# A two-layer hybrid DeltaNet trunk on one core: TensorE's order in the mixer fixed to the program's, the merges of two heads in lockstep, and the second short convolution ahead of the third head

## The chip, the cores and the metric

The kernel runs on one core of a Trainium2 chip. The metric is the device time of one execution in microseconds (us); the time given for a kernel is the median of several executions. A profile is one execution of the program, recorded instruction by instruction.

## What is computed

The trunk has two layers over 1024 positions of width 1024, all in float32. Cut to what matters here:

```python
def hybrid_layer(x, ...):
    h = rms_norm(x, norm1_g)
    proj = h @ w_in
    qkv, z, b_in, a_in, sc_in = ...split of proj...
    qkv = silu(causal_depthwise_conv(qkv, dn_conv_w))
    q, k = l2_normalize(q), l2_normalize(k)          # 4 heads of 128
    ...
    o_dn = chunk_gated_delta_rule(q, k, v, g, beta)  # a triangular solve per chunk, a scan over chunks
    o_dn = o_dn * rsqrt(mean(o_dn^2)) * dn_norm_g * silu(z)
    y = gate_b * causal_depthwise_conv(gate_c * hv, sc_conv_w)   # 4 groups of 128 channels
    o_sc = rms_norm over each group of y
    x = x + concatenate([o_dn, o_sc]) @ w_out
    h2 = rms_norm(x, norm2_g)
    return x + (silu(h2 @ ffn_w_gate) * (h2 @ ffn_w_up)) @ ffn_w_down
```

## The kernel before

**Matrix products.** Everything is held with channels on the 128 partitions and positions along the free axis, in two halves of 512 positions (half 0 and half 1). A float32 product is made of three passes: each operand is split into a rounded part `hi` (a copy on ScalarE) and the remainder `lo` (a subtraction on VectorE or GpSimd), and `mm3` (L205) issues hi·hi, hi·lo and lo·hi for each of the 8 slices of the 1024 input channels. One projection of 128 output channels over one half is 24 TensorE instructions of 128x512.

**One layer.** The mixer projects k, q and v for head 0 to 3 (`ps_k`, `ps_q`, `ps_v`), then z (`ps_z`, the gate of a head's output) and the three inputs of each short convolution group (`sconv`: `ps_csc`, `ps_hsc`, `ps_bsc`). Then come the output projection (`po`), gate and up (`P_g`, `P_u`), down (`P_d`), and a tail (`pd`) that adds the last four slices of the down projection.

**The delta rule beside the projections.** Its steps are small products of 128x128 and less. They are written as generators, "jobs": `tick()` is called behind every projection matmul, counts each job's lag down by one and, at zero, lets it trace its next step (`move`). For a head: transposes of k and q to tokens (`ktok`, `qtok`, L507), the Gram products `gk` and `gq` (L583, evacuated by VectorE as `U` and `A` in L584), the scaling of `kdec` by a decay (L588), and the transposes of v (`vtok`). For a group of two heads: `invert` inverts 32x32 triangles on VectorE or GpSimd over DRAM; after a further `INV_LAG` ticks `merge` (L639 to L663: `rp32`, `yp32`, `rp64`, `yp64`) makes 128x128 inverses `Y` from them, half by half and head by head; `chain` (L687 to L712) scans the chunks of both heads side by side: `kS`, `TR`, `SU` and the outputs `op`, with VectorE and ScalarE evacuating between; and the gate (L752) multiplies by z and stores to DRAM (`od`). The last steps of a group have no ticks left to wait for where the projections have run out: `drain()` then traces them at once.

**The output projection's operands.** For each half, eight tiles `ot` are loaded back from `od` (L1030, on SyncE's queue), the four of the short convolutions are scaled by `rb` (L1034), and each is split into `hhi_o` (L1035, ScalarE) and `hlo_o` (L1036, VectorE). `ot` takes the four SBUF buffers of tag `q`, which also hold the heads' q.

**What sets the order.** A scheduler orders each engine's instructions by the program's order and by when it thinks that their inputs are ready. `tc.issue_after(i)` keeps what is traced under it behind instruction `i`; before, only the jobs are under it, each behind the last projection matmul traced so far. So a projection may pass the jobs, and does. PSUM has eight banks: two for the projections (`mm`), `aux` and `fx` for transposes, Gram products and merges, `ch0` and `ch1` for the chain's short products, `o0` and `o1` for its outputs `op`.

## Time and profile before

| | |
|---|---|
| three executions | 2421.8, 2418.4 and 2419.73 us, median 2419.73 us |
| the profiled execution | 2423.16 us, of which the span of the trace is 2421.5 us |
| mean granted clock of TensorE | 0.987 |
| TensorE busy | 2340.7 us (97%) of the span |
| VectorE, ScalarE, GpSimd busy | 1622.2, 910.3 and 602.3 us (67%, 38%, 25%) |
| layer 0: mixer, `po`, gate and up, down, tail | begin at 4.8, 462.6, 552.8, 987.4 and 1166.1 us |
| layer 1: the same, and the end | begin at 1217.2, 1650.9, 1741.3, 2175.3 and 2353.8 us; ends at 2421.5 us |

The 1.66 us between the profiled execution's time and its span lie outside the trace. The stages' times are those of the first TensorE instruction of each.

### The profile page before, as it was taken

How to read it: one execution, taken by the hardware profiler on the slowest of the kernel's cores; microseconds unless marked ns; L12 is line 12 of the kernel's file. 1: busy time of each engine (PE TensorE's matmuls, PEld its weight loads, DVE VectorE, ACT ScalarE, POOL GpSimd, SP SyncE). 2: the span in 40 equal slices, each digit the busy share in tenths (PEclk: the TensorE clock that was granted, in tenths of full speed). 3: DMA queues.
4: the chain of work that ended last, by engine and by line, in shares of the span. 5: the costliest groups of instructions: out<-in, count | busy, mean ns of one | idle time of the engine just before them, and what ended most of it. 6: DMA issues, size and time to landing. Idle time of an engine off the chain costs nothing.

```text
span 2421.5 us, 31888 instructions
## 1 busy us (share of the span) xinstructions
PE 2340.7 (97%) x11522; PEld 1908.2 (79%) x11522; DVE 1622.2 (67%) x2870; ACT 910.3 (38%) x1917; POOL 602.3 (25%) x492
## 2 busy tenths in 40 slices
PE   7999999999999999999998999999999999999998
PEld 5787787887788888788777778878878888887877
DVE  7775773767655655799776666646685565568994
ACT  5524523534323223443344244234342322334334
POOL 3000000031444433234221001000325443422350
PEclk8999999999999999999999999999999999999999
DMA  7222223652333323744322312338423332346531
GB/s 228 66 65 71 65 63 90 204 183 61 109 118 105 113 87 98 248 144 146 106 69 71 76 49 69 77 92 251 124 75 119 106 113 87 109 137 220 160 101 70
DMA packets 362167, 275.21 MB, mean 114 GB/s; under 512 B 47343, under 2 KB 295449, under 8 KB 362009
## 3 DMA queue, kind: packets, MB, share of 16 engines
q1 hardware_dynamic: 362008, 273.18, 37.4%
q8 instruction: 90, 1.47, 0.3%
q14 instruction: 69, 0.56, 0.1%
HBM read 198.08 MB, written 75.04 MB: 113 GB/s over the span
## 4 chain that ended last, share of the span: by engine, by line
PE 73%; DVE 12%; issue 6%; DMA 4%; POOL 3%; ACT 2%; SPq 0%; DVEq 0%; POOLq 0%; ACTq 0%
PE P_g L205 16%; PE P_u L205 14%; PE P_d L205 7%; PE po L205 5%; PE ps_csc L205 4%; PE ps_bsc L205 4%; PE ps_hsc L205 4%; PE pd L205 3%; PE ps_v L205 3%; PE ps_z L205 2%; PE ps_k L205 2%; PE ps_q L205 2%; DMA stP<-hs_P 2%; DMA row<-gd 2%; DVE xT L1237 1%
## 5 line engine op out<-in xcount | busy, mean ns | idle before, releaser
L205 PE MATMUL P_g<-hi_hP,hi_P_g 128*128 128x512 f32 x608 | 239.5, 394 | 3.4 <-DVE u_g L995 1.9
L205 PE MATMUL P_g<-lo_hP,hi_P_g 128*128 128x512 f32 x608 | 238.7, 393 | 3.6 <-DVE lo_hP L898 3.6
L205 PE MATMUL P_u<-hi_hP,hi_P_u 128*128 128x512 f32 x608 | 237.6, 391 | 3.1 <-DVE c_g L1011 2.2
L205 PE MATMUL P_u<-lo_hP,hi_P_u 128*128 128x512 f32 x608 | 237.3, 390 | 0.0
L205 PE MATMUL P_u<-hi_hP,lo_P_u 128*128 128x512 f32 x608 | 237.1, 390 | 0.0
L205 PE MATMUL P_g<-hi_hP,lo_P_g 128*128 128x512 f32 x608 | 236.4, 391 | 0.0
L205 PE MATMUL P_d<-hi_dP,lo_P_d 128*128 128x512 f32 x504 | 196.8, 390 | 3.3 <-DVE lo_P_d L928 3.3
L205 PE MATMUL P_d<-hi_dP,hi_P_d 128*128 128x512 f32 x504 | 196.7, 390 | 2.2 <-ACT hi_dP L897 1.5
L205 PE MATMUL P_d<-lo_dP,hi_P_d 128*128 128x512 f32 x504 | 196.6, 390 | 0.9 <-DVE lo_dP L898 0.9
L205 PEld LDWEIGHTS P_g<-hi_hP,hi_P_g 128*128 128x128 f32 x608 | 114.9, 189 | 30.6 <-DVE u_g L995 2.8
L205 PEld LDWEIGHTS P_g<-lo_hP,hi_P_g 128*128 128x128 f32 x608 | 115.0, 189 | 28.7 <-DVE lo_hP L898 5.2
L205 PEld LDWEIGHTS P_u<-hi_hP,hi_P_u 128*128 128x128 f32 x608 | 114.6, 189 | 28.5 <-DVE c_g L1011 3.1
L205 PEld LDWEIGHTS P_g<-hi_hP,lo_P_g 128*128 128x128 f32 x608 | 114.9, 189 | 23.7
L205 PEld LDWEIGHTS P_u<-lo_hP,hi_P_u 128*128 128x128 f32 x608 | 114.7, 189 | 23.9
L205 PEld LDWEIGHTS P_u<-hi_hP,lo_P_u 128*128 128x128 f32 x608 | 114.4, 188 | 23.7
L1237 DVE TENSOR_TENSOR xT<-P_d,xT 128x512 f32<-128x512 f32 x192 | 125.1, 678 | 3.1 <-PE P_d L205 3.1
L927 ACT CAST hi_P_g<-m_g 128x1024 fp32r<-128x1024 f32 (+1 forms) x64 | 58.8, 919 | 151.9 <-PE P_u L205 127.7
L205 PEld LDWEIGHTS P_d<-hi_dP,lo_P_d 128*128 128x128 f32 x504 | 94.6, 188 | 25.0 <-DVE lo_P_d L928 5.8
L205 PEld LDWEIGHTS P_d<-hi_dP,hi_P_d 128*128 128x128 f32 x504 | 94.6, 188 | 23.6 <-ACT hi_dP L897 2.8
L205 PEld LDWEIGHTS P_d<-lo_dP,hi_P_d 128*128 128x128 f32 x504 | 94.6, 188 | 21.8 <-DVE lo_dP L898 2.2
L898 DVE TENSOR_TENSOR lo_dP<-stP,hi_dP 128x512 fp32r<-128x512 f32 x126 | 96.6, 790 | 18.0 <-ACT hi_dP L897 17.8
L897 ACT CAST hi_dP<-stP 128x512 fp32r<-128x512 f32 x126 | 75.2, 620 | 74.4 <-DMA stP<-hs_P 71.0
(410 smaller groups left out, 5872.0 us busy)
## 6 DMA issues: line engine op xcount, KB each, us to landing
stP<-hs_P SPq DMA_DIRECT2D x126, 256.0 KB, 3.8
m_g<-in_ffn_w_gate_dram SPq DMA_DIRECT2D x46, 512.0 KB, 4.1
m_u<-in_ffn_w_up_dram SPq DMA_DIRECT2D x44, 512.0 KB, 4.4
hs_P<-t SPq DMA_DIRECT2D x72, 256.0 KB, 2.4
m_d<-in_ffn_w_down_dram SPq DMA_DIRECT2D x48, 384.0 KB, 4.1
hs_P<-c_u SPq DMA_DIRECT2D x70, 256.0 KB, 2.0
raw_o<-in_w_out_dram SPq DMA_DIRECT2D x32, 512.0 KB, 4.8
xd<-xT SPq DMA_DIRECT2D x32, 256.0 KB, 2.3
```

The costliest lines, as they stand in the source:

```text
L205: last_mm[0] = PE.matmul(ps, lhsT=w(k)[i], rhs=m(k)[j], start=k + i + j == 0, stop=k + i == n).ins
L897: S.copy(res[0], src)
L898: eng.tensor_tensor(res[1], src, res[0].bitcast(F32), ALU.subtract)
L927: S.copy(hi, src)
L1237: V.tensor_tensor(t, ps, t, ALU.add)
```

## The change

In order of the diff: `LAG` goes from 6 to 8 and `INV_LAG` from 110 to 175 ticks, and tag `X` of the merges has two buffers. `mm3` puts each projection behind what was last traced on TensorE, and `move` does the same for each job, so that inside the mixer TensorE's order is the one in which the program traces it; only the first three projections of the kernel are free. For heads 0 and 1, whose work stands before any chain is running, `ktok`, `qtok`, `gk` and `gq` take the chain's banks `ch0`, `ch1`, `o0`, `o1` in place of `aux` and `fx`. The scaling of `kdec` moves from one VectorE instruction of 128x512 to four ScalarE activations of 128x128. The merges of a group's two heads go step by step side by side, one in `aux` and one in `fx`, and those of half 1 run beside the chain of half 0. The second short convolution comes before head 2. In the tail the splits of the down projection's weights are traced ahead of `tail_half(1)`, behind the last ScalarE copy of a split so far.

```diff
-LAG, TOK_LAG, SC_LAG, INV_LAG, GATE_LAG = 6, 36, 30, 110, 30
+LAG, TOK_LAG, SC_LAG, INV_LAG, GATE_LAG = 8, 36, 30, 175, 30
...
-    PB = {"tb": 1, "X": 1, "R": 2, "vn0": 1, "vn1": 1, "St": 6}
+    PB = {"tb": 1, "X": 2, "R": 2, "vn0": 1, "vn1": 1, "St": 6}
...
-    last_mm = [None]
+
+    last_mm, behind, strict = [None], [None], [True]
...
-                last_mm[0] = PE.matmul(ps, lhsT=w(k)[i], rhs=m(k)[j], start=k + i + j == 0, stop=k + i == n).ins
+                with tc.issue_after(behind[0]) if tick and behind[0] else nullcontext():
+                    mm = PE.matmul(ps, lhsT=w(k)[i], rhs=m(k)[j], start=k + i + j == 0, stop=k + i == n).ins
+                last_mm[0] = mm
+                behind[0] = mm if k + i == n and strict[0] else None
...
+            def side(hd, free, tag):
+
+                return lambda name, shape: ps_(free if hd < 2 else tag, name, shape)
...
             def move(job):
-                with tc.issue_after(last_mm[0]):
+                traced = nc.cur_bb.bb.instructions
+                n = len(traced)
+                with tc.issue_after(behind[0] or last_mm[0]):
...
+                for i in traced[n:]:
+                    if i.engine == last_mm[0].engine:
+                        behind[0] = i
...
+                strict[0] = l + hd + half > 0
...
-                ktok = transposed(u["k"], f"ktok_{nm}", aux)
+                ktok = transposed(u["k"], f"ktok_{nm}", side(hd, "ch0", "aux"))
...
-                V.tensor_tensor(u["kdec"], u["kdec"], u["kd"].unsqueeze(2).broadcast_to(sh4), ALU.mult)
+                for c in range(4):
+                    S.activation(u["kdec"][:, c, :], u["kdec"][:, c, :], AF.Copy, scale=u["kd"][:, c:c + 1])
...
-                vtok = transposed(u["v"], f"vtok_{nm}", aux)
+                vtok = transposed(u["v"], f"vtok_{nm}", (fx if hd < 2 and half else aux))
...
+                def merges(half):
+
+                    its = [merge(2 * g + i, half, i * 2 + half, (aux, fx)[i]) for i in range(2)]
+                    for lags in zip_longest(*its):
+                        yield LAG
+                yield from merges(0)
+                spawn(merges(1), 2 * LAG)
+                yield LAG
                 for half in range(2):
-                    for hd in (2 * g, 2 * g + 1):
-                        yield from merge(hd, half, (hd % 2) * 2 + half)
-                    yield LAG
                     yield from chain(g, half)
...
             sconv(0)
+            sconv(1)
             head(2, None)
             head(3, group(1))
-            for g in range(1, 4):
+            for g in range(2, 4):
...
+            with tc.issue_after(last_hi[0]):
+                wdn = [split_w(ffn_w_down[l][m * P:(m + 1) * P, :].rearrange("p (k c) -> p k c", c=P), f"d{l}_{m}",
+                               tags=None if m > tail[0] else ("ub", "yb")) for m in tail]
             tail_half(1)
```

**Merges on TensorE.** `rp` and `yp` are a merge's products, `X`, `R`, `Y` and `U` its operands; the names end in head, half, a number of the merge's step and a buffer number. In the order of before, the last `yp32` of the first merge, its `rp64` and its `yp64` stand like this:

```order
L648 MATMUL yp_0_0_0_1898<-Y_0_0_1869,R_0_0_0_1883 32x32 x2
L649 MATMUL yp_0_0_0_1898<-R_0_0_0_1883,Y_0_0_1869 32x32
L657 MATMUL rp_0_0_0_1920<-X_0_0_1870,U_0_0_1141 64x64 x4
L205 MATMUL ps_q_2_1_2236<-hhi_n_0_1_0_703,hi_q_2_2144 128x512
L205 MATMUL ps_q_2_1_2236<-hlo_n_0_1_0_704,hi_q_2_2144 128x512
L663 MATMUL yp_0_0_0_1933<-Y_0_0_1869,R_0_0_0_1925 64x64 x4
L205 MATMUL ps_q_2_1_2236<-hhi_n_0_1_0_703,lo_q_2_2145 128x512
```

In the order after, the first `rp32` of both heads of the same group and the first `yp32`:

```order
L652 MATMUL rp_0_0_0_1993<-X_0_0_1989,U_0_0_1141 32x32 x8
L652 MATMUL rp_0_1_0_2010<-X_1_0_2006,U_1_0_1522 32x32 x8
L208 MATMUL ps_hsc_1_0_1961<-hlo_n_0_0_5_418,hi_hsc_1_1922 128x512
L208 MATMUL ps_hsc_1_0_1961<-hhi_n_0_0_5_417,lo_hsc_1_1923 128x512
L208 MATMUL ps_hsc_1_0_1961<-hhi_n_0_0_6_423,hi_hsc_1_1922 128x512
L208 MATMUL ps_hsc_1_0_1961<-hlo_n_0_0_6_424,hi_hsc_1_1922 128x512
L208 MATMUL ps_hsc_1_0_1961<-hhi_n_0_0_6_423,lo_hsc_1_1923 128x512
L208 MATMUL ps_hsc_1_0_1961<-hhi_n_0_0_7_429,hi_hsc_1_1922 128x512
L208 MATMUL ps_hsc_1_0_1961<-hlo_n_0_0_7_430,hi_hsc_1_1922 128x512
L208 MATMUL ps_hsc_1_0_1961<-hhi_n_0_0_7_429,lo_hsc_1_1923 128x512
L661 MATMUL yp_0_0_0_2030<-Y_0_0_1988,R_0_0_0_2002 32x32 x2
```

Eight projection matmuls now stand between one step of the merges and the next, each step holds both heads, and the head-1 merge of half 0, which began 24 rows behind that of head 0, stands directly behind it. The same distance of eight stands ahead of `rp64` and `yp64`. From the last `vtok` of head 1 to the first `rp32` there are now 196 matmuls of 128x512, where there were 228.

**The end of the mixer on TensorE.** Before, the last step of the chain of heads 2 and 3 (half 1) is surrounded by z projections, and 67 matmuls of 128x512 stand from the last `op` of that chain to the first `po`:

```order
L687 MATMUL kS_3_1_3_4344<-S_3_1_2_4330,kT_k_3_1_2729 128x128
L691 MATMUL op_3_1_4179<-S_3_1_2_4330,qT_q_3_1_2964 128x128
L205 MATMUL ps_z_2_0_4303<-hhi_n_0_0_5_417,lo_z_2_4294 128x512
L205 MATMUL ps_z_2_0_4303<-hhi_n_0_0_6_423,hi_z_2_4293 128x512
L205 MATMUL ps_z_2_0_4303<-hlo_n_0_0_6_424,hi_z_2_4293 128x512
L205 MATMUL ps_z_2_0_4303<-hhi_n_0_0_6_423,lo_z_2_4294 128x512
L205 MATMUL ps_z_2_0_4303<-hhi_n_0_0_7_429,hi_z_2_4293 128x512
L205 MATMUL ps_z_2_0_4303<-hlo_n_0_0_7_430,hi_z_2_4293 128x512
L696 MATMUL TR_2_1_3_4355<-rr_2_1_3_4341,Y_2_1_4027 128x128
L696 MATMUL TR_3_1_3_4359<-rr_3_1_3_4346,Y_3_1_4096 128x128
L205 MATMUL ps_z_2_0_4303<-hhi_n_0_0_7_429,lo_z_2_4294 128x512
```

After, the z projections are over when the chain of half 0 ends, and the whole chain of half 1 stands among the first products of the output projection:

```order
L709 MATMUL TR_2_1_0_4430<-rr_2_1_0_4422,Y_2_1_4092 128x128
L709 MATMUL TR_3_1_0_4434<-rr_3_1_0_4427,Y_3_1_4109 128x128
L208 MATMUL po_0_0_4730<-hhi_o_0_3_4604,hi_o_0_4705 128x512
L717 MATMUL SU_2_1_0_4438<-vn_2_1_0_4432,kdec_2_1_2679 128x128
L725 MATMUL op_2_1_4418<-vn_2_1_0_4432,A_2_1_3114 128x128
L717 MATMUL SU_3_1_0_4443<-vn_3_1_0_4436,kdec_3_1_3187 128x128
L725 MATMUL op_3_1_4419<-vn_3_1_0_4436,A_3_1_3489 128x128
L208 MATMUL po_0_0_4730<-hlo_o_0_3_4605,hi_o_0_4705 128x512
L700 MATMUL kS_2_1_1_4448<-S_2_1_0_4440,kT_k_2_1_2556 128x128
L704 MATMUL op_2_1_4418<-S_2_1_0_4440,qT_q_2_1_2718 128x128
L700 MATMUL kS_3_1_1_4453<-S_3_1_0_4445,kT_k_3_1_3042 128x128
L704 MATMUL op_3_1_4419<-S_3_1_0_4445,qT_q_3_1_3206 128x128
L208 MATMUL po_0_0_4730<-hhi_o_0_3_4604,lo_o_0_4706 128x512
```

From the last z matmul to the last `op` of the chain there are 30 matmuls of `po`, most of them one to three at a time, which use the operands `hhi_o` and `hlo_o` one after the other as these are made. In the same stretch stand the transposes `ot` of the gates of half 0, whose result is stored to `od` and loaded again as the last two of the eight operands.

**The tail on VectorE.** `lo_d` is the remainder of a slice of the down projection's weights, `lo_f` that of a slice of the hidden activations. Before:

```order
L898 TENSOR_TENSOR lo_f_1_18_10335<-ft_1_18_10332,hi_f_1_18_10334 128x512
L1237 TENSOR_TENSOR xT_0_7_9044<-P_d_2_3_10307,xT_0_7_9044 128x512
L898 TENSOR_TENSOR lo_f_1_19_10341<-ft_1_19_10338,hi_f_1_19_10340 128x512
L898 TENSOR_TENSOR lo_f_1_20_10347<-ft_1_20_10344,hi_f_1_20_10346 128x512
L898 TENSOR_TENSOR lo_f_1_21_10353<-ft_1_21_10350,hi_f_1_21_10352 128x512
L1237 TENSOR_TENSOR xT_1_6_9042<-P_d_2_3_10318,xT_1_6_9042 128x512
L196 TENSOR_TENSOR lo_d_21_10377<-raw_d_21_10374,hi_d_21_10376 128x1024
```

After:

```order
L919 TENSOR_TENSOR lo_f_1_18_10383<-ft_1_18_10380,hi_f_1_18_10382 128x512
L1258 TENSOR_TENSOR xT_0_7_9068<-P_d_2_3_10331,xT_0_7_9068 128x512
L919 TENSOR_TENSOR lo_f_1_19_10389<-ft_1_19_10386,hi_f_1_19_10388 128x512
L197 TENSOR_TENSOR lo_d_21_10377<-raw_d_21_10374,hi_d_21_10376 128x1024
L1258 TENSOR_TENSOR xT_1_6_9066<-P_d_2_3_10342,xT_1_6_9066 128x512
L919 TENSOR_TENSOR lo_f_1_20_10395<-ft_1_20_10392,hi_f_1_20_10394 128x512
L919 TENSOR_TENSOR lo_f_1_21_10401<-ft_1_21_10398,hi_f_1_21_10400 128x512
```

The last `lo_d` stands three rows earlier, ahead of the last two `lo_f` and of an addition to `xT`. In both, `lo_k` of the next layer follows.

**Elsewhere on TensorE.** In the first group of each layer, `ktok` of head 1 stands ten rows behind `gk` of head 0 as it did, and `gk` of head 0's half 1 five rows behind that `ktok`; the first used to share one bank with the other (`aux`), and now `ktok` is in `ch0` and both `gk` are in `o0`. At the program's start, the transposes `bc_n` that spread the first norm's factors stood behind the first four transposes of `x`'s second half (`xtp`), and stand ahead of them. Counted over the whole order of a layer, a 128x512 matmul of the mixer and of `po` follows a smaller product 107 times, where it did 127 times in layer 0 and 125 times in layer 1.

## Rows read from the trace of the kernel before

**Rows 1.** The profile page, part 1: busy time, share of the span, instructions.

```profile
PE 2340.7 (97%) x11522; PEld 1908.2 (79%) x11522; DVE 1622.2 (67%) x2870; ACT 910.3 (38%) x1917; POOL 602.3 (25%) x492
```

**Rows 2.** Waits of TensorE, whole kernel: line, releaser, us in total, times, longest.

```profile
PE ktok L507 <- DVE U L584: 7.5, 2, 3.8
PE xtp L328 <- DMA xp<-in_x_dram: 5.8, 1, 5.8
...
PE pd L205 <- DVE lo_d L196: 4.7, 2, 2.3
PE ktok L507 <- DVE kT_k L483: 3.7, 3, 1.6
...
PE vtok L507 <- DVE v L597: 2.3, 3, 1.0
...
PE rp L657 <- DVE Y L653: 2.2, 2, 1.1
...
PE yp L648 <- ACT R L642: 1.8, 2, 0.9
...
PE vtok L507 <- DVE U L584: 1.5, 1, 1.5
```

**Rows 3.** Windows: length, busy (instructions) per engine, granted clock, DMA share, GB/s.

```profile
100.40:103.80 3.40, 2.92 (x10) 2.53 (x11) 3.02 (x6) 1.74 (x7) 0.00 (x0) 0.50 0.90 239
206.30:213.00 6.70, 6.70 (x28) 5.10 (x28) 2.31 (x4) 1.15 (x3) 0.00 (x0) 0.50 0.55 147
222.00:229.00 7.00, 6.49 (x47) 5.59 (x46) 5.10 (x13) 2.46 (x7) 0.00 (x0) 1.00 0.29 76
```

**Rows 4.** Timeline of VectorE, first Gram products: start, length, instruction, idle before.

```profile
96.70 1.29 DVE L588 TENSOR_TENSOR kdec<-kdec,kd 128x512 f32<-128x512 f32 x2
97.92 1.65 DVE L196 TENSOR_TENSOR lo_z<-raw_z,hi_z 128x1024 fp32r<-128x1024 f32 x1
...
100.15 0.68 DVE L584 TENSOR_TENSOR U<-gk,row 128x512 f32<-128x512 f32 x1
```

**Rows 5.** Timeline of ScalarE: eight scaled activations of 128x128.

```profile
451.72 2.18 ACT L728 ACTIVATE on<-op,mo 128x128 f32<-128x128 f32 x8 [1.14 <-DVE mo L724]
```

**Rows 6.** Timeline of VectorE at the program's start.

```profile
16.61 0.17 DVE L218 COPY rowr_n<-y_n 128x4 f32<-128x4 f32 x1
22.37 2.06 DVE L230 SCALAR_TENSOR_TENSOR ht_n<-xT,cst,bc_n 128x512 f32<-128x512 f32 x3 [5.59 <-PE bc_n L224]
```

**Rows 7.** Timeline of VectorE at layer 0's tail.

```profile
1166.00 3.46 DVE L898 TENSOR_TENSOR lo_f<-ft,hi_f 128x512 fp32r<-128x512 f32 x3
...
1169.98 1.21 DVE L196 TENSOR_TENSOR lo_d<-raw_d,hi_d 128x1024 fp32r<-128x1024 f32 x1
```

**Rows 8.** Timeline of TensorE in the chain: matmuls behind a small product, then products alone.

```profile
216.63 0.47 PE L205 MATMUL ps_q<-hhi_n,hi_q 128*128 128x512 f32 x1
216.94 0.39 PE L205 MATMUL ps_q<-hlo_n,hi_q 128*128 128x512 f32 x1
217.17 0.40 PE L205 MATMUL ps_q<-hhi_n,lo_q 128*128 128x512 f32 x1
...
222.34 0.39 PE L691 MATMUL op<-S,qT_q 128*128 128x128 f32 x2
222.56 0.39 PE L687 MATMUL kS<-S,kT_k 128*128 128x128 f32 x2
```

**Rows 9.** Tile `ot`: duration min, median, max in ns; then its load's landing.

```profile
L1035 ACT ACTIVATE hhi_o<-ot,cst x32: 707/725/736, 444.0 to 1673.1; 128x512 fp32r<-128x512 f32 x32
...
L1034 DVE TENSOR_TENSOR ot<-ot,rb x16: 679/684/693, 459.1 to 1669.6; 128x512 f32<-128x512 f32 x16
...
DMA to landing us min/median/max: 2.7/3.2/6.9
```

**Rows 10.** Timeline of TensorE, group 0's last transposes of v.

```profile
150.03 0.63 PE L507 MATMUL vtok<-ident,vT_v 128*128 128x128 f32 x4 [0.39 <-DVE v L597]
```

**Rows 11.** Timeline of SyncE's queue: the last load for group 0's merges.

```profile
190.84 0.99 SPq L633 DMA_DIRECT2D Y<-yd  x2
```

More of the change, by code (lines that the diff above doesn't have):

```diff
@@ L1 @@
-from contextlib import ExitStack
+from itertools import zip_longest
+from contextlib import ExitStack, nullcontext
 import concourse.bass as bass
@@ L359, in fx @@
                 return ps_("fx", name, shape)
-            def bank(tag):
-                return lambda name, shape: ps_(tag, name, shape)
+            def side(hd, free, tag):
+                return lambda name, shape: ps_(free if hd < 2 else tag, name, shape)
             def wcols(c0, n=P):
@@ L523, in query_tok @@
                 nm = f"{l}_{hd}_{half}"
-                qtok = transposed(units[hd, half]["q"], f"qtok_{nm}", fx)
+                qtok = transposed(units[hd, half]["q"], f"qtok_{nm}", side(hd, "ch1", "fx"))
                 sumsq(qtok, stat(hd)["ss"][:, 8 + half * 4:12 + half * 4], f"q_{nm}")
@@ L579, in gram @@
                 for src, dst in (("k", U), ("q", A)):
-                    gp = ps_({"k": "aux", "q": "fx"}[src], f"g{src}_{nm}", sh4)
+                    gp = {"k": side(hd, "o0", "aux"), "q": side(hd, "o1", "fx")}[src](f"g{src}_{nm}", sh4)
                     for c in range(4):
@@ L623, in invert, with merge @@
                     dma(diag_ap(yd[i]), yb[sl])
-            def merge(hd, half, slot):
+            def merge(hd, half, slot, bank):
                 nm = f"{l}_{hd}_{half}"
@@ L633, in merge @@
                 dma(Y, full_ap(yd[slot]))
-                rp = aux(f"rp32_{nm}", (P, 4, 32))
+                rp = bank(f"rp32_{nm}", (P, 4, 32))
                 for c in range(4):
@@ L643, in merge @@
                 yield LAG
-                yp = aux(f"yp32_{nm}", (P, 2, 4, 32))
+                yp = bank(f"yp32_{nm}", (P, 2, 4, 32))
                 for c in range(4):
@@ L654, in merge @@
                 yield LAG
-                rp = aux(f"rp64_{nm}", (P, 4, 64))
+                rp = bank(f"rp64_{nm}", (P, 4, 64))
                 for c in range(4):
@@ L660, in merge @@
                 yield LAG
-                yp = aux(f"yp64_{nm}", (P, 4, 64))
+                yp = bank(f"yp64_{nm}", (P, 4, 64))
                 for c in range(4):
@@ L889, in stats @@
                 return row_r(sp[:, 0:4], name)
+            last_hi = [None]
             def split(src, tags, name, eng=V):
@@ L896, in split @@
                                else sb(tag, nm, (P, HALF), F32R))
-                S.copy(res[0], src)
+                last_hi[0] = S.copy(res[0], src).ins
                 eng.tensor_tensor(res[1], src, res[0].bitcast(F32), ALU.subtract)
@@ L1276, in end @@
                     dma(out[0, ts_, :], xt)
+            with tc.issue_after(last_hi[0]):
+                wdn = [split_w(ffn_w_down[l][m * P:(m + 1) * P, :].rearrange("p (k c) -> p k c", c=P), f"d{l}_{m}",
+                               tags=None if m > tail[0] else ("ub", "yb")) for m in tail]
             tail_half(1)
-            wdn = [split_w(ffn_w_down[l][m * P:(m + 1) * P, :].rearrange("p (k c) -> p k c", c=P), f"d{l}_{m}",
-                           tags=None if m > tail[0] else ("ub", "yb")) for m in tail]
             acc = [[sb("pre", f"acc1_{l}_{h}")] for h in range(2)]
```

## Prediction

> **What bounds the kernel now.** I read the page's busy times first: TensorE is busy 2340.7 of 2421.5 us, and no other engine over 67% [rows 1]. So the time is TensorE's own work plus what it waits plus what it loses at the lower clock. Its own work hardly changes (the same products), so I went to its waits over the whole kernel, then to windows of the granted clock, and last to timelines around the waits in question. The list of waits shows that nearly 81 us of idle time are many short waits, and which of them lie in the mixer and in the tail, where the diff acts [rows 2]. The windows show a second price: behind some waits the granted clock is 0.50, the 1.2 GHz level, for 3.4 or 6.8 us [rows 3], and half of such a stretch is lost. A 128x512 matmul follows another by 0.23 us, and comes 0.31 us behind small products [rows 8], so each return from small products costs 0.09 us more.
>
> Gate, up and down keep their order, and I cost them at nothing: their waits lie outside the edits.
>
> **First Gram products of each layer.** `ktok` waits for `U` twice, 7.5 us [rows 2]: it needs `aux`, which `gk` holds until VectorE has written `U`, and VectorE first does two `kdec` passes (1.28 us start to start) and `lo_z` (1.65) [rows 4]. With `ktok` in another bank that wait goes. The next to need a bank of the Gram products is `gk` of half 1, in `o0`. `U` would end at 100.83 − 1.28 = 99.55 us; TensorE gets to that `gk` one `ktok` (0.45) and four matmuls (1.0) after 96.9, at 98.3. So 1.2 us of wait are left there, and up to 2.1 with `gq`, which waits for `A`, one VectorE pass later. I take 1.7 for each layer: 7.5 − 3.4 = 4.1 us gained. Layer 0's wait also ends in 3.4 us at half clock [rows 3]; a wait of 1.7 probably doesn't bring that, so 1.7 more. **Gain 5.8** (2 to 9).
>
> **kdec on ScalarE.** Four activations of 128x128 cost about 4 × 0.27 = 1.1 us (eight took 2.18) [rows 5], 16 times in the kernel, 17 us on an engine that is busy 38% [rows 1]. `kdec` is read first by `SU`, after the whole inversion. I cost it at nothing; without that cover it would be 1.1 us a time.
>
> **Merges.** TensorE waits 1.8 us for `R` and 2.2 for `Y` [rows 2], once in each layer each, and then runs 6.7 us at half clock in layer 0 [rows 3]; layer 1 has the same pair of waits and the same length of low clock. Together 4.0 + 2 × 3.35 = 10.7 us. In the new order eight matmuls, 1.8 us, stand between the steps, against waits of 0.9 and 1.1 each. Two heads' evacuations now queue on VectorE ahead of `rp64`, so a few tenths may be left. **Gain 9** (0 to 10.7).
>
> **Small waits in the heads.** `vtok` on `v` 2.3 and on `U` 1.5 [rows 2] go, with two banks for `vtok` and with `U` earlier. Of the three waits of `ktok` on `kT` (3.7 [rows 2]) the longest, 1.6, has thirteen matmuls ahead of it now where it had one. The other two belong to heads 2 and 3, where `aux` and `fx` stay as they were: there I expect a wait on `U` of 1.7 in each layer in place of such a wait and of one of `ot`, about as long together. 2.3 + 1.5 + 1.6 and 0.8 for what these pairs leave: **gain 6.2** (3 to 7).
>
> **Returns from small products.** 20 fewer in layer 0 and 18 in layer 1, at 0.09 us: **gain 3.4**.
>
> **Start.** The row of norm factors is ready at 16.8, yet VectorE waits 5.59 us for `bc` until 22.37 [rows 6], because TensorE stands at `xtp` for its DMA (5.8 us [rows 2]) ahead of `bc`. With `bc` first, `ht` can start some 3.6 us earlier; the other `xtp` still stand ahead of the first projection and still wait for their loads. **Gain 2.5** (0 to 3.6).
>
> **Tail.** `pd` waits 4.7 us for `lo_d`, twice 2.3 [rows 2], which on VectorE stands behind three `lo_f` and an `xT` [rows 7]. Two of the `lo_f` and the `xT` come later now, 2.9 us at 1.15 and 0.6 each, more than the wait. Each wait is followed by 3.4 us at half clock, as in the first of [rows 3]. 4.7 + 2 × 1.7 = **gain 8** (4.7 to 8.1). The `lo_f` of slice 20 and 21 come 1.1 us later; TensorE reaches them after the slices before, six matmuls later.
>
> **The end of the mixer: a new wait.** Before, 67 matmuls stood between the chain's end and `po`; after, none. From the moment at which the chain's half 0 has read its last q, the new order has 41 matmuls of 128x512 (9.3 us, 13 returns 1.2), 44 products at 0.22 us [rows 8] (9.7) and eight transposes (0.7): 21 us of TensorE work. In the same stretch the eight `ot` of half 0 go through the only two `q` buffers that are free then (the other two hold q of half 1). A round of two is a load of 3.2 us, a multiplication by `rb` of 0.68 for half of them, a `hhi` of 0.73 [rows 9] and a last VectorE pass of about 0.7: 4.6 or 5.3. Four rounds make 19.8, and the last two loads wait for a store from the gate, 2.7 at least if it is as quick as the quickest load [rows 9]: 22.5. VectorE and ScalarE take their work in order and evacuate the chain in between; where the chain ran without cover, VectorE was busy 5.10 of 7.00 us [rows 3], so I add 4: 26.5. That is 5.5 us of waiting in each layer, and 1.5 for one short drop of the clock. **Loss 14 in all** (0 to 35). Behind the blocked `ot` loads on SyncE's queue stand loads of the later weights, needed 30 us later, so they cost nothing unless the rounds take twice that.
>
> For these loads the Trainium skill, DMA: Bandwidth & Descriptors, section Anatomy of one DMA, gives about 2.0 us plus the bytes over 436 GB/s, fitted on another queue than SyncE's; worked out, an estimate of 2.6 us for 256 KB. The trace shows 2.7 at the least and 3.2 in the middle, so I keep the row; by the page's figure the four rounds would be 2.4 us shorter in each layer, and the forecast 2394.
>
> **Sum.** 5.8 + 9 + 6.2 + 3.4 + 2.5 + 8 − 14 = 20.9 us. The profiled execution took 2423.16, 1.66 more than its span, so 2402.3 for one like it; it lies 3.4 above the median of the runs, so the median comes to 2399.
>
> **Rivals.**
> *The end of the mixer hides its loads* (0.15). If two more buffers come free sooner or VectorE isn't in the way, the loss is near 0: gain 35, 2385. For it: 21 us of work against 22.5. Against it: every operand is used as soon as it is made.
> *The waits move instead of going* (0.22). The fixed order can't step round a late input. 196 matmuls behind the last `vtok` (150.03 [rows 10]) are 45 us, so `rp32` comes at about 196; the last loads for the merges were issued until 191.8 [rows 11] and land 2.7 to 3.2 later. That leaves 1 to 2 us, and the old order had 228 matmuls, 52 us. If the inversion is 3 us later, or VectorE is late with `Y`, then the merges' 9 and 3 of the Gram products' gain are lost: gain 9, 2411.
> *Loads at the end of the mixer at their slow end* (0.09), the one on the other side. A load has taken up to 6.9 us [rows 9]; 3.7 more in four rounds is 15 us a layer on top of 5.5, and a long wait drops the clock, 3.4 lost as behind the merges [rows 3]. Then the loss is 2 × 24 = 48 against 35 gained: 2433. It turns to slower from a loss of 20 us a layer, rounds of some 9 us. Against it: other queues are nearly idle there.
> *The clock stays low through the hand-over* (0.06): 21 us of work in scraps between waits, at 1.2 GHz, would be up to 21 us longer in each layer, 15 if a third of it fills the waits: a loss of 2 × 22, 2428. Against it is the stretch 222 to 229 us, the same chain products with hardly a matmul between, at a clock of 1.00 [rows 3]. The Trainium skill, Perfetto Trace Analysis, section Matmul Optimizations, says that TensorE scales with its utilization and that matmuls should come back to back in batches; by that rule this interleaving is bad, and that row speaks against it so long as waits stay short.
>
> **How the numbers follow.** A difference under 0.2% (4.8 us) can't be told from none here. My forecast has 0.48; its own range is 2390 to 2408, from the hand-over's 22.5 or a landing 1 us longer, and half of the merges' gain. For 8 in 10 the range takes in the hidden loads and the moved waits, 2381 to 2417, and leaves out the two slow cases. Faster: 0.48 + 0.15 + two thirds of 0.22, which is 0.78; same: the rest of that, and 0.03 of the slow ones in a milder form, 0.10; slower 0.12.
>
> **What would show it.** In the profile after: no wait of `ktok` on `U` at head 1, and one under 2 us of `gk` on `U`; no waits inside the merges, and a clock of 1.00 behind them; no `pd` wait on `lo_d`; `bc` in front of the first `xtp`; waits of `po` on `hlo_o` or `ot` of some 5 us in each layer, in the 27 us from the last z on. I am wrong if `rp` waits for `X`, if the `po` waits sum to over 10 us a layer, or if the clock is at 0.50 for more than 7 us there.

## The result, and the profile after

The changed kernel takes 2402.39 us (median of 4 executions, 2401.91 to 2411.86) against 2420.76 us of the kernel before (4 executions on the same chip, 2418.4 to 2421.8): a ratio of 0.9935, 95% interval 0.9909 to 0.9961. The profiled execution took 2401.96 us, its span is 2400.2 us, 21.3 less than before. The forecast was 2399 with a range of 2381 to 2417; its own narrower range, 2390 to 2408, holds the median too.

The first part of the page after, to be held against [rows 1]:

```profile
PE 2320.3 (97%) x11522; PEld 1906.1 (79%) x11522; DVE 1622.6 (68%) x2854; ACT 925.8 (39%) x1981; POOL 601.3 (25%) x492
```

This one line already says that the sum was right for partly wrong reasons. TensorE was idle 2421.5 − 2340.7 = 80.8 us before and is idle 2400.2 − 2320.3 = 79.9 us now. Nearly all of the gain stands in its busy time, which fell by 20.4 us with the same 11522 matmuls; the forecast had nearly all of it in waits and clock. (Busy time also holds what the low clock costs while TensorE works; that share is taken apart below.)

The waits of TensorE after, whole kernel, to be held against [rows 2] (line, releaser, us in total, times, longest):

```profile
PE ot L519 <- ACT on L741: 9.0, 4, 2.7
PE po L208 <- ACT hhi_o L1056: 6.5, 2, 3.4
...
PE ktok L519 <- DVE v L610: 2.8, 2, 1.4
...
PE bc_n L229 <- DVE rowr_n L223: 2.6, 1, 2.6
...
PE ot L519 <- DVE z_z L765: 2.0, 2, 1.0
...
PE xtp L333 <- DMA xp<-in_x_dram: 1.8, 1, 1.8
PE gk L595 <- ACT sqk L514: 1.8, 2, 0.9
...
PE vtok L519 <- DVE v L610: 1.4, 2, 0.8
...
PE SU L717 <- ACT vn L711: 1.3, 2, 0.6
PE ktok L519 <- DVE kT_k L494: 1.2, 1, 1.2
...
PE po L208 <- DVE hlo_o L1057: 0.9, 2, 0.5
PE pd L208 <- DVE lo_d L197: 0.9, 2, 0.5
```

The waits of `ktok` on `U`, of `rp` on `Y` and of `yp` on `R` are gone, and that on `lo_d` is a fifth of what it was. In their place stand waits that [rows 2] doesn't show: `ot` on `on` and `z_z`, `ktok` on `v`, `gk` on `sqk`, and `po` on `hhi_o`.

Where the busy time fell is seen in windows over the whole span that count only the merges' tiles. Before, `rp` and then `yp` (length, busy time of TensorE, of its weight loads, and of the engines behind):

```profile
0.00:2421.50 2421.50, 21.80 (x384) 16.22 (x384) 14.69 (x48) 0.99 0.38 114
0.00:2421.50 2421.50, 19.68 (x512) 15.16 (x512) 20.29 (x64) 0.99 0.38 114
```

And after:

```profile
0.00:2400.20 2400.20, 14.68 (x384) 12.69 (x384) 14.47 (x48) 0.99 0.38 115
0.00:2400.20 2400.20, 14.73 (x512) 12.74 (x512) 20.29 (x64) 0.99 0.38 115
```

The busy time of the same 896 small products is 41.5 us before and 29.4 after, 12.1 less. Not all of that is gained: the busy time of a batch also covers stretches in which the next matmul already runs, and two of the broken batches in each layer stood at half clock before. Counted from the trace in another way, each matmul from its start to the next one's start, without idle time and with half of the low-clock stretches taken off, the merges cost 34.1 us before and 27.2 after, 6.9 less. They now come in unbroken batches of two heads, 32 of them where there were 78 pieces. A timeline of one such batch of 32 `rp32` products, with the matmul ahead of it and the one behind (start, length):

```profile
189.85 0.39 PE L208 MATMUL ps_hsc<-hhi_n,hi_hsc 128*128 128x512 f32 x1
190.16 0.69 PE L652 MATMUL rp<-X,U 32*32 32x32 f32 x32
190.79 0.50 PE L208 MATMUL ps_hsc<-hlo_n,hi_hsc 128*128 128x512 f32 x1
```

The 32 products take 0.69 us. Before, 16 at the most stood together, and such a batch took 0.44; others were broken up by projections and by products of the chain.

The same way of counting shows where the rest went. Over the whole kernel TensorE's work took 2314.6 us before and 2298.6 after, 16.0 less: 6.9 from the merges, 8 from matmuls of 128x512 and about 1 from the other small products. The 8 lie beside the small products: the 128x512 matmuls that stand directly before or behind one took 32.1 us more than 0.227 us each before, and 23.6 after.

The windows that answer to [rows 3]: the whole merge stretch of layer 0's first group, and the place where `po` now waits:

```profile
195.00:222.00 27.00, 27.00 (x258) 22.77 (x257) 10.11 (x26) 6.45 (x23) 0.00 (x0) 1.00 0.13 37
...
438.80:442.20 3.40, 0.41 (x2) 0.00 (x0) 1.65 (x8) 0.39 (x1) 0.00 (x0) 1.00 0.53 171
442.20:445.60 3.40, 3.02 (x10) 2.63 (x11) 1.76 (x3) 3.00 (x10) 0.00 (x0) 0.50 0.75 190
```

TensorE is busy without a gap through the merges and the chain behind them, at a clock of 1.00; the 6.7 us at half clock are gone. At the end of the mixer a gap of 3.4 us is followed by 3.4 us at half clock. The timelines of ScalarE, SyncE's queue and TensorE there say what the gap is made of:

```profile
441.81 0.72 ACT L1056 ACTIVATE hhi_o<-ot,cst 128x512 fp32r<-128x512 f32 x1 [4.66 <-DVE ot L1055]
...
436.30 2.00 SPq L1051 DMA_DIRECT2D ot<-od  x2
...
442.58 0.80 PE L208 MATMUL po<-hhi_o,hi_o 128*128 128x512 f32 x1 [3.38 <-ACT hhi_o L1056]
```

The second pair of `ot` loads is issued at 436.30; ScalarE stands idle 4.66 us for it, and TensorE 3.38. Layer 1 has the same wait, 3.1 us.

### The profile page after: what moved, and what is told of

It reads as the page before. It is cut to its first block, busy times and chain, and to the rows that moved or that the text cites. A ratio compares the mean times of both kernels' runs of the same rounds, so it can differ in the third digit from the quotient of the medians.

```text
span 2400.2 us, 31952 instructions
## 1 busy us (share of the span) xinstructions
PE 2320.3 (97%) x11522; PEld 1906.1 (79%) x11522; DVE 1622.6 (68%) x2854; ACT 925.8 (39%) x1981; POOL 601.3 (25%) x492
## 4 chain that ended last, share of the span: by engine, by line
PE 79%; DVE 9%; DMA 4%; issue 3%; ACT 2%; POOL 2%; SPq 0%; DVEq 0%; POOLq 0%; ACTq 0%
PE P_g L208 16%; PE P_u L208 15%; PE P_d L208 9%; PE po L208 6%; PE ps_z L208 4%; PE ps_bsc L208 4%; PE ps_hsc L208 4%; PE ps_csc L208 4%; PE pd L208 3%; PE ps_v L208 3%; PE ps_k L208 3%; PE ps_q L208 2%; DMA stP<-hs_P 1%; DVE xT L1258 1%; DMA ot<-od 1%
## 5 line engine op out<-in xcount | busy, mean ns | idle before, releaser
L208 PE MATMUL po<-hhi_o,hi_o 128*128 128x512 f32 x256 | 101.5, 400 | 6.7 <-ACT hhi_o L1056 6.5
```

The lines of the kernel that those rows point to most:

```text
L208: mm = PE.matmul(ps, lhsT=w(k)[i], rhs=m(k)[j], start=k + i + j == 0, stop=k + i == n).ins
```

## The experiments

Two theories stood against each other. The one of the forecast: the time comes from waits and drops of the clock that the banks, the distances and the tail's order remove, less a new wait at the hand-over from mixer to `po`. The other comes from the profile after: the waits mostly move, and what is saved is TensorE's own running (its busy time less what the low clock costs), because its small products stay together. A third question was which of the edits carries the gain, and a fourth whether the hand-over can be had for less. All ratios are to the kernel before, run in the same set on the same chip. Not undone by themselves were `INV_LAG`, the second buffer of `X`, the place of the second short convolution and the merges of half 1 beside the chain; what each of them is worth stays open.

### The changed kernel again

No edit; it stands in one set with the lockstep experiment, the gate's lag and the third tile of the hand-over experiments.

> The changed kernel itself, beside the others of this set: 0.9935 of the kernel before, as measured, with 0.0025 to either side; 2402 to 2406 on this chip's scale. It is here so that differences of 3 to 6 us between variants are not those of chips.

2404.64 us, 0.9949 [0.9936, 0.9961]. Two profiled executions of one kernel thus differ by 6.2 us of span (2400.2 and 2406.4), and it is the clock: the mean granted clock is 0.989 in one and 0.985 in the other, idle time 79.9 and 78.2. Over all executions of this set the mean clock is 0.9872 for the changed kernel (5) and 0.9878 for the kernel before (11). So the clock brought nothing here, though it looks like a gain when the first two profiles alone are compared (0.989 and 0.987).

### The fixed order, with the new banks and with the old

Without the fixed order (first), with the fixed order and the old banks (second), and with neither (both edits):

```diff
-                with tc.issue_after(behind[0]) if tick and behind[0] else nullcontext():
+                with nullcontext():
...
-                behind[0] = mm if k + i == n and strict[0] else None
+                behind[0] = None
...
-                for i in traced[n:]:
-                    if i.engine == last_mm[0].engine:
-                        behind[0] = i
```

```diff
-                return lambda name, shape: ps_(free if hd < 2 else tag, name, shape)
+                return lambda name, shape: ps_(tag, name, shape)
...
-                vtok = transposed(u["v"], f"vtok_{nm}", (fx if hd < 2 and half else aux))
+                vtok = transposed(u["v"], f"vtok_{nm}", aux)
```

> The changed kernel with TensorE's order left to the scheduler again: projections under no wait on order, jobs only behind the last projection traced, all else as changed (banks, lockstep, lags, kdec, second short convolution early, tail). If the banks, the distance of eight and the tail do the work, as in my account, the time is 2400 to 2406, since eight ticks still stand between the merges' steps in the program. Rival (the fixed order itself brings the gain): merges and transposes stand together again with waits of about 1 us each and the clock falls behind the merges, 8 us or more: 2410 to 2416.

> The changed kernel with ktok, qtok, gk, gq and vtok of all heads in aux and fx, as before. My account (the shared bank makes the wait): ktok of head 1 waits for U again, by 2.5 us in each layer (3.8 less the 1.3 us of kdec that VectorE no longer does first), and vtok for v again, 1 to 2 us a layer; with a drop of the clock 5 to 10 us in all: 2407 to 2412. Rival (taking kdec from VectorE cured it): under 2 us, 2402 to 2404.

> The changed kernel with TensorE's order left to the scheduler and with the old banks (aux and fx for every transpose and Gram product): the fourth corner beside the changed kernel (fixed, new banks: 0.9949), the free order with new banks (0.9953) and the fixed order with old banks (1.0051). If the fixed order only does harm where a bank is late and the scheduler steps round such waits, this lies between, 2408 to 2414. Rival (the old banks cost the same 27 us in any order): 2428 or more.

| | new banks | old banks |
|---|---|---|
| fixed order | 0.9949 [0.9936, 0.9961] | 1.0051 [1.0039, 1.0063], 2432.13 us |
| free order | 0.9953 [0.9941, 0.9965], 2407.5 us | 0.9990 [0.9980, 1.0000], 2415.28 us |

(Upper left: the run of the changed kernel in the second set; its first was 0.9935.) With the new banks the fixed order can't be told from none; with the old ones it costs 1.0051 − 0.9990, some 15 us, and makes the kernel slower than before. I had priced the old banks at 5 to 10 us and they cost some 25. The waits of the kernel with the old banks show how:

```profile
PE gps L423 <- DVE y L421: 9.6, 2, 5.2
...
PE ktok L519 <- DVE v L610: 5.6, 4, 1.4
PE xtp L333 <- DMA xp<-in_x_dram: 5.5, 1, 5.5
...
PE vtok L519 <- DVE v L610: 3.3, 6, 0.9
...
PE gk L595 <- ACT sqk L514: 3.3, 4, 0.9
```

`gps` and `gtp` (running sums of the decays, and their transpose) use bank `fx`, and `gps` needs `y`, which VectorE makes in a long chain of short steps. With the old banks the transposes `qtok` of head 0 need `fx` too and are traced behind `gtp`, and in the fixed order the projections stand behind `qtok`. So TensorE stood 5.2 us in layer 0 until `y` was there, and `qtok` came at 71.03 us. With the new banks `qtok` comes at 65.67, `gps` at 72.65 with projections between, and it waits 0.4; with the old banks in the free order it waits 0.5. The `xtp` wait of [rows 2] is back too: it is 5.5 and 5.8 us with the old banks and 1.8 and 1.6 with the new (fixed and free order). Why the banks of the heads decide on this was not tried.

### The merges one head after the other

```diff
-                    its = [merge(2 * g + i, half, i * 2 + half, (aux, fx)[i]) for i in range(2)]
-                    for lags in zip_longest(*its):
+                    for i in range(2):
+                        yield from merge(2 * g + i, half, i * 2 + half, aux)
                         yield LAG
```

> The changed kernel with the merges of the two heads one after the other in aux, as before, but still eight ticks between their steps, TensorE's order still the program's, and the merges of half 1 still beside the chain of half 0. If the eight matmuls between the steps are what covers the merges' waits (my account), no wait inside the merges comes back and only the chain starts four steps of eight ticks, 7 us of projections, later: more of it falls among the first output projections, 2 to 6 us over the changed kernel. Rival (lockstep in two banks is what removes the waits): the waits of yp on R and of rp on Y of about 1 us come back eight times over and the clock falls, 10 us or more.

2408.12 us, 0.9960 [0.9947, 0.9973], against 0.9949 [0.9936, 0.9961] in the same set: no difference that can be told. Yet the profile differs. First the page's busy times, then the merges' tiles `rp` and `yp`, then two of its waits:

```profile
PE 2335.2 (97%) x11522; PEld 1909.3 (79%) x11522; DVE 1612.4 (67%) x2854; ACT 927.4 (39%) x1981; POOL 602.9 (25%) x492
```

```profile
0.00:2406.40 2406.40, 18.48 (x384) 14.45 (x384) 14.72 (x48) 0.99 0.38 114
0.00:2406.40 2406.40, 19.02 (x512) 14.92 (x512) 20.26 (x64) 0.99 0.38 114
```

```profile
PE yp L661 <- ACT R L655: 4.3, 2, 2.2
...
PE ot L519 <- ACT on L741: 2.4, 3, 0.9
```

The merges' busy time is 37.5 us instead of 29.4 (31.1 instead of 27.2 from start to start, without idle time and low clock), and in return `ot` waits 2.4 for `on` instead of 7.6 (9.0 in the first profile). Inside the merges there is hardly a wait either, but for one `yp` of 2.2 us in each layer at the end of the mixer, where the projections have run out and no matmul stands between `rp` and `yp`; in layer 0 it is followed by 10.2 us at half clock. So lockstep kept the merges clear of that place. Elsewhere it removed no wait that the distance of eight had left; it saved running, and other waits took it back.

The two directions become plain when all profiles stand side by side. Busy and idle are from each page and span; half of the time at the low clock, (1 − granted clock) × span, is taken off the busy time (the clock is given to a thousandth, so to some 1 us; where the clock is low while TensorE idles, this takes off too much). The last column is the busy time of the merges' tiles.

| kernel | span | busy | clock | busy without the clock's loss | idle | merges |
|---|---|---|---|---|---|---|
| before | 2421.5 | 2340.7 | 0.987 | 2309.2 | 80.8 | 41.5 |
| changed | 2400.2 | 2320.3 | 0.989 | 2293.9 | 79.9 | 29.4 |
| changed, again | 2406.4 | 2328.2 | 0.985 | 2292.1 | 78.2 | 29.4 |
| free order, new banks | 2401.5 | 2329.5 | 0.991 | 2307.9 | 72.0 | 38.3 |
| free order, old banks | 2413.2 | 2332.2 | 0.990 | 2308.1 | 81.0 | 38.3 |
| fixed order, old banks | 2426.4 | 2329.1 | 0.986 | 2295.1 | 97.3 | 29.5 |
| merges one by one | 2406.4 | 2335.2 | 0.988 | 2306.3 | 71.2 | 37.5 |
| changed, `LAG` 6 (below) | 2391.3 | 2318.0 | 0.990 | 2294.1 | 73.3 | 29.4 |

With the loss taken from the trace only where TensorE is busy, the fourth column reads 2314.6, 2298.6, 2299.3, 2312.7, 2315.8, 2301.3, 2310.9 and 2299.6: other numbers, the same two groups of kernels. Fixed order and lockstep together bring TensorE's running from some 2308 us to 2294 (by the second count from 2311 to 2316 down to 2299 to 2301); either alone doesn't. The new banks take 9 us of idle time in a free order and 17 to 19 in a fixed one. The fixed order adds 6 to 8 us of idle time with the new banks and 16 with the old. What is left is a kernel with 15 us less running and the same idle time. But the saved running is not time that only this kernel could gain: in the free order with the new banks the running is within 2 us of the kernel before, and it was as fast as the changed one, with 9 us less idle time than before and fewer low-clock stretches (mean clock 0.9888 over 6 executions, against 0.9874 over 11 of the kernel before). There the forecast's waits and clock are what pays.

### The tail's order undone

```diff
-            with tc.issue_after(last_hi[0]):
-                wdn = [split_w(ffn_w_down[l][m * P:(m + 1) * P, :].rearrange("p (k c) -> p k c", c=P), f"d{l}_{m}",
...
             tail_half(1)
+            wdn = [split_w(ffn_w_down[l][m * P:(m + 1) * P, :].rearrange("p (k c) -> p k c", c=P), f"d{l}_{m}",
```

> The changed kernel with the weight splits of the tail traced behind tail_half(1) again, as before. My account (the tail's gain is lo_d standing ahead of two lo_f): both waits of pd on lo_d of about 2.3 us come back, with 3.4 us at half clock behind each, so 4.7 to 8 us over the changed kernel: 2407 to 2410. Rival (the tail became shorter by what is ahead of it, since its earlier wait on xT fell too): the waits stay at 0.5 us and the time within 2 us of 2402.

2410.72 us, 0.9961 [0.9950, 0.9973]. The wait is back:

```profile
PE pd L208 <- DVE lo_d L197: 4.7, 2, 2.3
```

The two tails take 51.1 and 67.9 us, as before, where the changed kernel has 48.0 and 65.1: 5.9 us for this edit, by the stages' own times. By the ratios it is 3 to 6 us (0.9961 against 0.9949 and 0.9935).

### kdec scaled on VectorE again

```diff
-                for c in range(4):
-                    S.activation(u["kdec"][:, c, :], u["kdec"][:, c, :], AF.Copy, scale=u["kd"][:, c:c + 1])
+                V.tensor_tensor(u["kdec"], u["kdec"], u["kd"].unsqueeze(2).broadcast_to(sh4), ALU.mult)
```

> The changed kernel with the scaling of kdec on VectorE again, one pass of 0.64 us from start to start in place of four activations. My account: U comes 1.3 us later, so gk of half 1 waits for it by 1 to 1.5 us in each layer where the changed kernel shows no wait, 2 to 4 us over the changed kernel. Rival (cover of the nine matmuls ahead of gk is enough): no wait, within 2 us.

2411.43 us, 0.9975 [0.9966, 0.9983], 12 executions; against 0.9949 [0.9936, 0.9961] of another set some 6 us, where I expected 2 to 4. The waits:

```profile
PE ot L519 <- ACT on L740: 13.5, 4, 3.7
...
PE gk L595 <- DVE U L596: 1.2, 1, 1.2
```

The wait of `gk` for `U` that I had priced appears only here, 1.2 us in one layer; most of the difference is in `ot`, whose operand `on` comes later (13.5 us against 9.0 and 7.6). VectorE has 16 more passes in the heads here, which may be why; that was not traced back.

### Other covers for the hand-over

First the loads of `ot` in buffers of tag `U` (the first edit of the diff alone); then the same with the operands of half 1 traced behind the third (`d == 2`) or the fifth (`d == 4`) tile of `po`:

```diff
-                    ot = sb("q", f"ot_{nm}_{k}")
+                    ot = sb("U", f"ot_{nm}_{k}")
...
-            for half in range(2):
+            def operands(half):
...
+            operands(0)
...
+                    if half * KD + d == 2:
+                        operands(1)
```

> The changed kernel with the ot tiles of the output projection in the four buffers of tag U, which the last merge frees, in place of tag q. My account (eight loads through two free buffers make the wait of po on hhi_o of 3.1 to 3.4 us, with 3.4 us at half clock behind it, in each layer): that wait and that drop go, 7 to 10 us: 2393 to 2395. Rival (VectorE and ScalarE, busy with the chain's evacuations, are what is late): the loads land early, the wait stays over 2 us, and the time is within 3 us of 2402.

> The changed kernel with the ot tiles in the buffers of tag U, and those of half 1 loaded from behind the third output projection on, so that no load of them stands ahead of the loads of x on SyncE's queue. If that queue is what gave the 8 us wait of po on xh in the run with U alone, it goes, and with it the waits of po on hhi_o: 0.3 to 2 us of waiting per layer there, 8 to 11 us under the changed kernel. Rival (po waits for VectorE, which the chain fills): waits of 4 us or more remain in each layer and the time is within 3 us of the changed kernel.

> The changed kernel with the ot tiles in tag U and those of half 1 loaded from behind the fifth output projection on, in place of the third. In the run with the third, po waited for xh by 3.8 and 2.8 us in the middle of the output projection, since VectorE stood at the half-1 operands. If their place in VectorE's order is what makes it, these waits go: 5 to 8 us under that run, 0.990 to 0.992 of the kernel before. Rival: the operands are then late for the second half of the output projection, with a wait of po on hlo_o or hhi_o of 3 us or more a layer, and nothing is gained.

With the buffers alone: 2406.82 us, 0.9949 [0.9937, 0.9960], where I expected 2393 to 2395. The wait for `hhi_o` shrinks from 6.5 us to 4.4, so other buffers take away only a part of it, and a greater one appears, 14.7 us in the two layers. SyncE's queue, and TensorE behind it (`xo` is the residual x that is loaded for an addition, `xh` the sum):

```profile
449.03 5.53 SPq L1051 DMA_DIRECT2D ot<-od  x5
...
458.27 0.90 SPq L1082 DMA_DIRECT2D xo<-xd  x2
...
468.00 0.79 PE L208 MATMUL po<-hhi_o,hi_o 128*128 128x512 f32 x1 [8.02 <-DVE xh L1083]
```

The `ot` of half 1 now stand on SyncE's queue ahead of `xo`, which the first half's evacuation needs. With half 1 behind the third tile the wait is less than half of that:

```profile
PE po L208 <- DVE xh L1086: 6.6, 2, 3.8
```

2399.95 us, 0.9924 [0.9910, 0.9938]: some 6 us better than the changed kernel in its set (0.9949), with intervals that just touch, where I expected 8 to 11. Behind the fifth tile the wait for `xh` is 1.8 us, but the operands of half 1 are too late, 2432.5 us, 1.0061 [1.0046, 1.0075], where I expected a gain. The wait, and the window from the first of these waits:

```profile
PE po L208 <- ACT hhi_o L1057: 28.2, 13, 4.3
```

```profile
501.30:521.80 20.50, 12.01 (x22) 6.78 (x23) 7.22 (x10) 5.50 (x8) 0.00 (x0) 0.50 0.28 83
```

So the slow side of the hand-over is real: thirteen waits of up to 4.3 us in the two layers, and in each a stretch of 20.5 us at a clock of 0.50, the 1.2 GHz level.

### The gate's lag

```diff
-LAG, TOK_LAG, SC_LAG, INV_LAG, GATE_LAG = 8, 36, 30, 175, 30
+LAG, TOK_LAG, SC_LAG, INV_LAG, GATE_LAG = 8, 36, 30, 175, 44
```

> The changed kernel with GATE_LAG 44 in place of 30: 14 ticks more, 3.2 us, between a chain's end and the transposes of its gate. In the fixed order these transposes (ot) wait for ScalarE's on by 1.8 us and then for z by 1.0 in each layer at the start of head 3. If the place in the order makes the wait, both go, and the drop of the clock behind it in one layer: 5 to 8 us under the changed kernel. Rival (ScalarE is late there however far back they stand, since the norm's sums queue with the heads' work): the waits stay or move to ktok and gk of head 3, within 2 us.

2407.31 us, 0.9958 [0.9946, 0.9970], no better than the changed kernel, where I expected 5 to 8 us. The waits of `ot` on `on` fall to 5.2 us, and those on `z_z` rise to 5.2:

```profile
PE po L208 <- ACT hhi_o L1056: 7.6, 2, 4.2
PE ot L519 <- DVE z_z L765: 5.2, 4, 1.8
```

In a fixed order these waits move along the row; a later gate doesn't remove them.

### A lag of six, as before the change

```diff
-LAG, TOK_LAG, SC_LAG, INV_LAG, GATE_LAG = 8, 36, 30, 175, 30
+LAG, TOK_LAG, SC_LAG, INV_LAG, GATE_LAG = 6, 36, 30, 175, 30
```

> The changed kernel with LAG 6 as before: six matmuls, 1.4 us, between the steps of merges and chain. In the kernel before the waits inside a merge were 0.9 and 1.1 us with nothing between; 1.4 us cover these for one head, less surely for two. If cover is what counts, small waits (under 0.5 us each) come back in merges and chain, and the chain of half 1 begins 7 us of projections earlier, so the end of the mixer loses less: within 4 us of the changed kernel, either way. Rival (eight is needed): waits of 0.5 us or more at each of the 16 steps, over 6 us more.

2393.01 us (2390.58 to 2397.61), 0.9901 [0.9886, 0.9916]: the best version of all, and some 12 us under the changed kernel by its second run (0.0048 of 2419 us; the intervals lie apart, in different sets), 8 us by its first (0.9935, whose wider interval overlaps a little). I had it within 4 us. The waits on which it differs, and the second pair of `ot` loads on SyncE's queue:

```profile
PE ot L519 <- ACT hi_q L196: 4.4, 2, 2.2
...
PE po L208 <- DVE hlo_o L1057: 1.7, 2, 0.9
...
PE ot L519 <- ACT on L741: 0.3, 1, 0.3
```

```profile
431.60 2.08 SPq L1051 DMA_DIRECT2D ot<-od  x2
```

The running is that of the changed kernel (table above: 2294.1, merges 29.4), and the merges wait for nothing here either. What is gained lies in the output projection: from its first matmul to the first of the gate projection it takes 105.9 and 108.5 us in the two layers, against 111.2 and 112.8 in the changed kernel; that is 9.6 us together, where the spans differ by 8.9. My account: the chain, which has one such distance at every step, ends sooner, and with it the hand-over. In the trace the second pair of `ot` loads is issued at 431.60 instead of 436.30, while the first `po` matmul comes only 0.6 us sooner (433.8 and 434.4). The wait of `po` for `hhi_o` is gone, and the waits of `ot` for `on` nearly so. Idle time accounts for 5 to 7 us of the gain; the mean clock, 0.9900 over 5 executions against 0.9872, goes with it.

## Why the prediction was right, step by step

The sum of 20.9 us met the 21.3 between the two profiles by luck, through errors that cancel; by the medians the gain is 18.4 us, and 13.0 in the second set (2417.69 before, 2404.64 after). By the forecast, 10.5 us came from waits (4.1 + 4.0 + 6.2 + 2.5 + 4.7 − 11), some 7 from the clock and 3.4 from returns. Measured in the two profiles: 0.9 from waits, 4 to 5 from the clock, 15 to 16 from TensorE's running. The part of the clock isn't even firm: in the changed kernel's second profile the low clock costs 3 to 5 us more than before, and over the executions of that set the mean clock is no higher (0.9872 and 0.9878). The drops that the forecast named are gone, and others came.

- **"Its own work hardly changes (the same products)" failed.** The products are the same; their running isn't. The merges' products fell by 6.9 us from start to start, and the 128x512 matmuls beside small products by 8.5, where the forecast had 3.4 for the returns alone. That price was too small because it counted only the matmul behind a small product: 38 fewer returns at the 0.09 us that the trace bears out are 3.4, but matmuls ahead of a small product, and those between two, cost more too. It takes the fixed order and lockstep both, and the view that would have shown it was there before: the size of the merges' batches and the time of the matmuls beside them.
- **First Gram products: right, and more (5.8).** The 7.5 us on `U` are gone with no residue, and so is the 3.4 us at half clock. The residue I had left, 1.7 a layer, isn't there: `U` starts at 97.44, not the 98.87 that I had, because VectorE does `lo_z` sooner, and `gk` comes at 98.53, about as worked out. (Two `kdec` passes are 1.22 us from start to start in [rows 4], not 1.28; nothing hangs on it.) With `kdec` on VectorE 1.2 of it show.
- **kdec on ScalarE (0): right for ScalarE**, whose busy time rose by 15.5 us (17 forecast). What it takes off VectorE is worth some 6 us, which I had credited in the Gram step alone.
- **Merges (9): right in waits and clock**, 4.0 us and two stretches of 6.8 at half clock. But the lockstep isn't what removed these waits: with merges one by one at a distance of eight they stay away too, but for the one `yp` in each layer at the end of the mixer. In lockstep a distance of six is enough; six with merges one by one in the fixed order was not run.
- **Small waits in the heads (6.2): wrong in sign.** `vtok`, `ktok` on `kT` and `v`, and `ot` on `sqk` summed to 9.8 us before (2.3 + 1.5 + 3.7 + 0.2 + 2.1, the last two from the list of waits). The same steps with `gk` on `sqk`, `ot` on `z_z` and the share of `ot` on `on` that lies in the heads (3.6) sum to 12.8. Every operand that is a little late now stops the row (in the free order with the new banks `ot` waits 0.9 us for `on` in the whole kernel, here 9.0). That is the mechanism of the rival "the waits move", at another place than I gave it: `rp` never waits for `X` (the last one landed at 188.4, `rp32` began at 190.16, the margin of 1 to 2 us that I had worked out).
- **Start (2.5): at most 0.9.** `bc` does go first, and `xtp` waits 1.8 instead of 5.8; but 2.6 appear at `bc_n`, and the first `ktok` begins at 40.0 us before and at 39.9 after (39.1 in the changed kernel's second profile). Why the rest is lost on the way to it was not tried.
- **Tail (8): the mechanism right, the size 5.9** by the stages. A wait of 0.5 on `lo_d` is left in each layer.
- **The hand-over (−14): the mechanism right, the size some 18.** `po` waits 7.4 us (6.5 + 0.9), less than the 11 forecast; 5.4 us of `ot` on `on` and 0.5 more of `SU` come in, and three stretches of 3.4 us at half clock: some 18 in all. The waits of `ot` for `on` were not in the forecast. The rounds of loads were a cause as worked out: other buffers for `ot` shorten that wait (6.5 to 4.4) and bring another, and at a distance of six, where the loads start sooner, it is gone.

Of the rivals, hidden loads didn't come (waits of 3 us in each layer), nor loads at their slow end, nor a clock low throughout. For the loads the trace after has:

```profile
DMA to landing us min/median/max: 2.6/3.4/4.7
```

The estimate from the Trainium skill, DMA: Bandwidth & Descriptors, section Anatomy of one DMA, 2.6 us for 256 KB, is the quickest load here and not the middle one, so the row was the better price. In the hand-over the clock is at half for 3.4 us behind a wait of 3.4 in the changed kernel, and for 20.5 us with the operands of half 1 too late; products scattered among projections without waits kept a clock of 1.00. The rule of the Trainium skill, Perfetto Trace Analysis, section Matmul Optimizations, that TensorE scales with its utilization and so matmuls should come back to back in batches, thus agrees with the stretches in which waits crowd together; for scattered products without waits this trace doesn't bear it out. The shorter running of whole batches stands with the low clock taken off, so it is another matter than this rule.

## What to carry to other kernels

Before an order is fixed, look for every operand and every bank that is late by a little: a free order steps round it, a fixed one pays it with all that stands behind. Here the fixed order cost 15 us with shared banks (1.0051 against 0.9990), and with banks of their own for the first heads it was no better and no worse than the free one (0.9949 and 0.9953). Look at busy time as well as at waits: small products that are kept together in one batch cost TensorE less for the same count, themselves and in the large matmuls beside them, and idle time can stay as it was while the kernel gets faster. Compare the clock over many executions, not over two profiles. Try a distance between dependent steps as small as the evacuation allows: each one lengthens the chain, and where the next stage's loads wait for the chain's end, that stage starts later. Six instead of eight gave 0.9901 against 0.9949 and 0.9935, at least half as much again as the whole change had brought; these are the only two distances that were run, so the best one is open.

## What was not expected of the hardware

From start to start, without idle time and low clock, the 896 merge products took 34.1 us of TensorE in broken batches, 31.1 in whole batches of one head and 27.2 in whole batches of two; 16 more products added only 0.25 us to a 32x32 batch (0.44 and 0.69). From its start to the next, a 128x512 matmul took 0.227 us among its like, 0.32 behind a small product, and 0.24 to 0.26 ahead of one. And the clock's drops differ between executions of one kernel, with nearly the same idle time: 0.989 and 0.985 on average, some 7 us of TensorE's busy time at half clock.
